# Two tiles of a scaled matrix product leave in four transfers of 6, 5, 12 and 105 rows

## The chip, the cores and the metric

The kernel runs on one core of a Trainium2 chip. A core has a matrix engine (PE), three engines for elementwise work (DVE, ACT, POOL, the last also called GpSimd), and a sequencer (SP, SyncE) that does no arithmetic and here issues transfers. Transfers between the chip's main memory (HBM) and the core's on-chip memory (SBUF, 128 partitions) are carried out by 16 DMA engines that the core's issuing engines share. The metric is the device time of one execution in microseconds; the profile's span runs from the first to the last recorded instruction and is a little shorter.

## The reference

```python
batch, m, k, n = 16, 512, 1024, 768        # all float32, scale = 0.1
def reference(x, weight, scale, add_value):
    return (scale * np.matmul(x, weight) + add_value).astype(np.float32)
```

The batch is flattened: 8192 rows of x times a 1024 by 768 weight, times 0.1, plus an array of the shape of the result.

## The kernel before

The 8192 rows are 64 tiles of 128 rows. Tiles are grouped in blocks of 24, 24 and 16, and inside a block a partition holds neighbouring rows of memory, so that a transfer of n tiles is, on each of 128 partitions, one contiguous run of n times 3 KB (of the result or the added array) or n times 4 KB (of x). A "row" of a transfer below is such a run on one partition: a transfer of two tiles of the result has 128 rows of 6 KB.

SP issues all transfers, in the order written out in STREAM. A word such as `a56+8` names the operand (x, w for weight, a for the added array, o for the result), the first tile and the number of tiles. In front of each transfer SP waits for what it needs (the helper `need`): a load for its buffer to be free, a store for the semaphore `made` to say that the tiles have been finished. Each transfer counts one semaphore up by 16 when its data have landed. The last word, `o62+2`, is left out of this loop and is issued after the block in which all engines run their programs, when all of them have reached its end.

The loaded tiles of x lie in 16 slots (`xs`). ACT and POOL each run `mover`: moves of four tiles, in which they cast x from float32 to bfloat16 into one of two buffers (`va`), each engine half of the casts, eight of them to a move and engine (sixteen half-sized ones in the first two moves). DVE transposes the result of a move, two tiles at a time, into `xt` (L190). PE multiplies: eight chunks of the contraction for each tile, a 512-wide and a 256-wide matmul for each chunk (L248, L222). DVE then scales the product, adds the loaded array and writes the sum over it in `ao` (L199), two tiles at a time, and counts `made` up. `ao` has 32 tile slots; it holds the added array first, then the result, and the stores read it.

The mover's first four moves are written out; the remaining twelve are a loop of three iterations with four moves each, in which the wait for the loaded tiles and the wait for a free `va` buffer take their values from the loop's register. POOL's last move, tiles 60 to 63, is the last move of the last iteration.

Tiles 46 and 47 are stored as part of `o32+16`, the transfer of 16 tiles late in STREAM:

```python
... x60+4 a52+4 a56+8 o32+16 o48+8 o56+6 o62+2
```

## Time and profile before

| | |
|---|---|
| time, median of 3 runs | 209.41 us (209.21 to 209.54) |
| the profiled execution's own time | 209.42 us |
| its span | 207.6 us |
| what lies around the span | 1.8 us |
| PE busy | 170.7 us (82%) |
| DVE busy | 123.0 us (59%) |
| ACT busy | 137.8 us (66%) |
| POOL busy | 138.3 us (67%) |
| packets of the hardware queue, as a share of 16 engines' span | 98.0% |

How to read it: the DMA share is a mean over the 16 DMA engines, so that one engine alone at work shows as about 0.06. A packet is one row of a transfer, or the small write by which a DMA engine reports its part of the transfer. For a stretch of time the share counts the packets that start in it. A DMA line of the profile's part on issues gives the median time from the issue to the landing of the whole transfer. Issuing a transfer is not counted as busy time of the issuing engine.

### The profile page before, as it was taken

How to read it: one execution, taken by the hardware profiler on the slowest of the kernel's cores; microseconds unless marked ns; L12 is line 12 of the kernel's file. 1: busy time of each engine (PE TensorE's matmuls, PEld its weight loads, DVE VectorE, ACT ScalarE, POOL GpSimd, SP SyncE). 2: the span in 40 equal slices, each digit the busy share in tenths (PEclk: the TensorE clock that was granted, in tenths of full speed). 3: DMA queues.
4: the chain of work that ended last, by engine and by line, in shares of the span. 5: the costliest groups of instructions: out<-in, count | busy, mean ns of one | idle time of the engine just before them, and what ended most of it. 6: DMA issues, size and time to landing. Idle time of an engine off the chain costs nothing.

```text
span 207.6 us, 2250 instructions
## 1 busy us (share of the span) xinstructions
PE 170.7 (82%) x1024; PEld 50.8 (24%) x512; DVE 123.0 (59%) x66; ACT 137.8 (66%) x145; POOL 138.3 (67%) x148
## 2 busy tenths in 40 slices
PE   0001993699999999999999999999999899999800
PEld 0000230123223333333333333333333233333200
DVE  0038304937677767776777677767774867777320
ACT  2494199999596969696969079999696959100000
POOL 0399299999797969696969179999796959200000
PEclk9999999699999999999999999999999999999995
DMA  6999999999999999899999999999999999998994
GB/s 224 458 432 410 448 455 404 455 455 404 404 473 436 420 388 505 350 421 440 436 431 447 404 450 459 404 420 436 436 421 428 412 455 469 455 445 355 434 420 173
DMA packets 4034, 87.05 MB, mean 419 GB/s; under 512 B 448, under 2 KB 448, under 8 KB 576
## 3 DMA queue, kind: packets, MB, share of 16 engines
q1 hardware_dynamic: 4032, 87.03, 98.0%
q14 instruction: 2, 0.02, 0.0%
HBM read 61.87 MB, written 25.17 MB: 419 GB/s over the span
## 4 chain that ended last, share of the span: by engine, by line
PE 59%; DMA 26%; POOL 5%; DVE 4%; issue 2%; SPq 0%; DVEq 0%; POOLq 0%
PE mm L248 39%; PE mm L222 20%; DMA xs<-in_x_dram 11%; DMA out_dram<-ao 10%; DMA ao<-in_add_value_dram 5%; POOL va L166 5%; DVE xt L190 2%; DVE ao L199 2%; SPq L99 0%; SPq L102 0%; DVEq L199 0%; DVEq L196 0%; POOLq L160 0%; DVEq L188 0%; SPq L292 0%
## 5 line engine op out<-in xcount | busy, mean ns | idle before, releaser
L248 PE MATMUL mm<-w_bf,xt 128*128 128x512 bf16 x512 | 170.3, 385 | 26.0 <-DVE w_bf L183 20.2
L166 POOL CAST va<-xs 32x1024 bf16<-32x1024 f32 (+1 forms) x144 | 138.1, 959 | 39.1 <-DMA xs<-in_x_dram 18.6
L166 ACT CAST va<-xs 32x1024 bf16<-32x1024 f32 (+1 forms) x144 | 136.5, 948 | 38.4 <-DMA xs<-in_x_dram 20.5
L222 PE MATMUL mm<-w_bf,xt 128*128 128x256 bf16 x512 | 141.4, 276 | 0.0
L199 DVE SCALAR_TENSOR_TENSOR ao<-mm,ao 128x1536 f32 (+1 forms) x32 | 56.2, 1755 | 58.7 <-PE mm L222 46.2
L248 PEld LDWEIGHTS mm<-w_bf,xt 128*128 128x128 bf16 x512 | 50.8, 99 | 145.4 <-issue 138.4
L190 DVE STREAM_TRANSPOSE xt<-va 128x1024 f32<-128x1024 f32 x32 | 65.2, 2037 | 16.9 <-POOL va L166 16.9
L183 DVE CAST w_bf<-ao 128x3072 bf16<-128x3072 f32 x2 | 4.3, 2170 | 0.0
L153 ACT ACT_TABLE_LOAD x1 | 1.3, 1283 | 1.3 <-SPq L255 1.3
L278 POOL MEMSET const-float32-0.0<- 128x1 f32 x1 | 0.1, 98 | 0.2 <-issue 0.2
L278 POOL MEMSET const-bfloat16-1.0<- 128x1 bf16 x1 | 0.1, 100 | 0.0
L278 POOL MEMSET const-uint8-127<- 128x1 uint8 x1 | 0.1, 98 | 0.0
L278 POOL MEMSET const-float32-1.0<- 128x1 f32 x1 | 0.1, 97 | 0.0
## 6 DMA issues: line engine op xcount, KB each, us to landing
xs<-in_x_dram SPq DMA_DIRECT2D x6, 4096.0 KB, 20.5
ao<-in_add_value_dram SPq DMA_DIRECT2D x7, 3072.0 KB, 17.0
out_dram<-ao SPq DMA_DIRECT2D x5, 3072.0 KB, 22.4
xs<-in_x_dram SPq DMA_DIRECT2D x4, 2048.0 KB, 14.3
out_dram<-ao SPq DMA_DIRECT2D x1, 6144.0 KB, 29.9
ao<-in_weight_dram SPq DMA_DIRECT2D x1, 3072.0 KB, 14.0
ao<-in_add_value_dram SPq DMA_DIRECT2D x2, 1536.0 KB, 9.9
out_dram<-ao SPq DMA_DIRECT2D x1, 2304.0 KB, 11.5
```

The source lines that it names most:

```text
L153: eng.preload_act_table(mybir.ActivationFunctionType.Copy)
L166: copied = copy(va[q % VA_BUFS][32 * b:32 * b + 32, t:t + step, a, :], src[32 * a:32 * a + 32, t:t + step, b, :])
L183: eng.tensor_copy(w_bf[:, s:s + n, :], ao[:, s:s + n, :]).then_inc(casts, n)
L190: eng.transpose(xt[:, 2 * half:2 * half + 2, :, :].rearrange("p i c (a m) -> p i c a m", a=4), pairs.rearrange("p i a (k c) -> p i c a k", ...
L199: eng.scalar_tensor_tensor(a, mm[:, q:q + 2, 0:N], float(scale), a, op0=mybir.AluOpType.mult, op1=mybir.AluOpType.add).then_inc(made, 2)
L222: return eng.add_instruction(mybir.InstMatmult(name=nc.get_next_instruction_name(), engine=eng.engine, ins=[eng.lower_ap(weights), eng.low ...
L248: eng.matmul(mm[:, q, 0:CUT], piece, w_bf[:, j, 0:CUT], **flags)
L278: nc = _bacc.Bacc("TRN2", target_bir_lowering=False, num_devices=1)
```

## The change

`o32+16` becomes `o32+14`. The result of tiles 46 and 47, 128 rows of 6 KB, leaves in four transfers instead, cut by partitions: the first 6 rows from SP, right behind `o32+14`; then 5, 12 and 105 rows from POOL, one after the other, between its last two moves, once `made` says that tile 47 is finished. Each of the four has a semaphore of its own, and ACT waits for all four at the end of its program. So that POOL's transfers can stand ahead of its last move, the mover's loop is turned by one move: three moves are written out ahead of it, its iterations hold the moves of slots 3, 0, 1, 2, and the last move stands behind it. The number of moves and of casts stays the same, for ACT too. SP, which issued every transfer before, shares that with POOL.

```diff
+SPREAD = 46
+SPREAD_ROWS = (("SP", 6), ("Pool", 5), ("Pool", 12), ("Pool", 105))
-    ... a52+4 a56+8 o32+16 o48+8 o56+6 o62+2
+    ... a52+4 a56+8 o32+14 o48+8 o56+6 o62+2
+    spread_sem = [tc.alloc_semaphore(f"spread{i}") for i in range(len(SPREAD_ROWS))]
+
+    def spread(eng, name):
+        first = 0
+        for (by, n), sem in zip(SPREAD_ROWS, spread_sem):
+            if by == name:
+                eng.dma_start(rows(out_v, SPREAD, 2)[first:first + n],
+                              ao[first:first + n, slots(SPREAD, 2), :]).then_inc(sem, 16)
+            first += n
+        assert first == P
...
             transfer(eng, op, s, n).then_inc(sem, 16)
+            if op == "o" and last == SPREAD:
+                need(made, MADE + SPREAD + 2)
+                spread(eng, "SP")
...
-        for q in range(X_SLOTS // MOVE):
+        for q in range(3):
             move(q, MOVE // 2 if q in HALVED else MOVE, 16,
                  MOVE * (q + 1) if q >= VA_BUFS else None)
-        with eng.Fori(32, T + 1, X_SLOTS) as i:
-            for q in range(X_SLOTS // MOVE):
-                move(q, MOVE, i, i + (4 * q - 12) if q < 3 else i)
+        with eng.Fori(16, T, X_SLOTS) as i:
+            move(3, MOVE, i, i)
+            for q in range(3):
+                move(q, MOVE, i + 16, i + 4 * (q + 1))
+        if go is not None:
+            eng.wait_ge(made, MADE + SPREAD + 2)
+            spread(eng, "Pool")
+        move(3, MOVE, T, T)
+        if go is None:
+            for sem in spread_sem:
+                eng.wait_ge(sem, 16)
```

More of the change, by code (lines that the diff above doesn't have):

```diff
@@ L20 @@
 FETCH = 128
+SPREAD = 46
+SPREAD_ROWS = (("SP", 6), ("Pool", 5), ("Pool", 12), ("Pool", 105))
 STREAM = """
     x0+4 w0+8 x4+8 a0+8 x12+4 a8+8 x16+8 a16+8 x24+8 a24+8 x32+8 o0+8 o8+8 a32+8 x40+8
-    a40+8 x48+8 x56+4 o16+8 o24+8 a48+4 x60+4 a52+4 a56+8 o32+16 o48+8 o56+6 o62+2
+    a40+8 x48+8 x56+4 o16+8 o24+8 a48+4 x60+4 a52+4 a56+8 o32+14 o48+8 o56+6 o62+2
 """
```

## The prediction

> **What bounds the kernel now.** I read the page first, then a table of stretches with the DMA share, then the packets of the last microseconds one by one. From the page:

> ```profile
> span 207.6 us, 2250 instructions
> DMA  6999999999999999899999999999999999998994
> DMA packets 4034, 87.05 MB, mean 419 GB/s; under 512 B 448, under 2 KB 448, under 8 KB 576
> q1 hardware_dynamic: 4032, 87.03, 98.0%
> ```

> The transfers fill the span: 16 DMA engines are busy 98.0% of it, and only the first and the last of the 40 slices are visibly short. The packets also tell how a transfer is shared out. 28 transfers of 128 rows would give 3584 packets; the page has 4032, and the 448 small ones are 28 x 16. So each DMA engine takes 128/16 = 8 rows of a transfer and adds one small packet.

> Stretch by stretch (start:end, length, busy times, granted clock, DMA share, GB/s):

> ```profile
> 2.00:26.00 24.00, 5.83 (x23) 1.56 (x12) 8.20 (x4) 11.30 (x19) 13.26 (x18) 1.00 1.00 424
> 100.00:140.00 40.00, 40.00 (x248) 12.06 (x124) 28.21 (x16) 31.46 (x31) 30.83 (x31) 1.00 1.00 431
> 177.00:190.00 13.00, 13.00 (x82) 3.91 (x41) 10.02 (x6) 0.45 (x1) 0.70 (x1) 1.00 1.00 433
> 190.00:198.00 8.00, 6.70 (x42) 1.88 (x20) 3.05 (x3) 0.00 (x0) 0.00 (x0) 1.00 0.99 426
> 203.40:203.80 0.40, 0.00 (x0) 0.00 (x0) 0.00 (x0) 0.00 (x0) 0.00 (x0) 0.50 1.06 445
> 203.80:204.20 0.40, 0.00 (x0) 0.00 (x0) 0.00 (x0) 0.00 (x0) 0.00 (x0) 0.50 0.95 399
> 204.20:204.60 0.40, 0.00 (x0) 0.00 (x0) 0.00 (x0) 0.00 (x0) 0.00 (x0) 0.50 0.81 338
> 204.60:205.00 0.40, 0.00 (x0) 0.00 (x0) 0.00 (x0) 0.00 (x0) 0.00 (x0) 0.50 0.38 154
> 205.00:205.20 0.20, 0.00 (x0) 0.00 (x0) 0.00 (x0) 0.00 (x0) 0.00 (x0) 0.50 0.08 31
> 205.20:205.40 0.20, 0.00 (x0) 0.00 (x0) 0.00 (x0) 0.00 (x0) 0.00 (x0) 0.50 0.07 31
> 205.40:206.20 0.80, 0.00 (x0) 0.00 (x0) 0.00 (x0) 0.00 (x0) 0.00 (x0) 0.50 0.05 23
> ```

> All engines of the DMA work without a break from 2 us to 203.8 us; then they fall out one after the other, and from 205.0 us on the share is that of one engine in 16. That one engine sets the end. Its packets, first from 205.0 us and then from 205.2 us (bins of 0.075 and 0.07 us):

> ```profile
> DMA  0100100100100100000000000000000000000000
> DMA packets 9, 0.03 MB, mean 10 GB/s; under 512 B 4, under 2 KB 4, under 8 KB 9
> DMA  0200020020020000000000000000000000000000
> DMA packets 5, 0.02 MB, mean 9 GB/s; under 512 B 1, under 2 KB 1, under 8 KB 5
> SPq L292 <- DMA out_dram<-ao: 7.5, 1, 7.5
> out_dram<-ao SPq DMA_DIRECT2D x1, 768.0 KB, 7.9
> ```

> Five rows start after 205.0 us, one behind the other; from the first to the fourth start after 205.2 us it is 10 bins for three rows, 0.23 us a row. The fifth starts at about 205.97 us and ends at about 206.20 us. The other three small packets lie between 205.0 and 205.2 us: three more engines are done only there, the other 12 earlier. The last DMA wait of SP (7.5 us, L292) is for exactly this store, `o62+2`, 7.9 us from issue to landing. So the last engine is about 206.20 - 205.15 = 1.05 us behind the next. PE, DVE, ACT and POOL do nothing in that time.

> **The change part by part.** The sum is made against the profiled execution, 209.42 us (span 207.6 and 1.8 around it), which is 0.01 from the median of 209.41.

> *What the last engine loses.* The 128 rows of tiles 46 and 47 came as 8 to each engine. The change is said to leave engine 4 three. Nothing in the profile numbers the engines, so whether the last one is engine 4 is an assumption, and so is the sharing out of the pieces; 5 rows fewer is 5 x 0.23 = 1.15 us, and the profile has just five rows alone at the end. The bounds: at most all 8 rows go (-1.84); with four pieces it may also get more (below).

> *What the others gain.* Five rows must go elsewhere. If they go singly, five engines have 9 rows, 0.23 us later. If one of the three that end by 205.2 us is among them (chance 1 - (10 x 9 x 8)/(15 x 14 x 13) = 0.74, were the five drawn from 15), the new end of the rows is about 205.15 + 0.23 = 205.38 instead of 206.20: a gain of 0.82. If none is, the last engine's own 206.20 - 1.15 = 205.05 and the others' 205.15 leave 1.05. I take 0.82, the likelier.

> [...] No run here shows a transfer of other than 128 rows.

> *Smaller rows and more packets.* Rows of 48 KB (177 to 190 us) move at 433 GB/s, the 6 KB and 18 KB ones (203.4 to 203.8 us) at 445 with whole packets counted at their start, and 24 KB ones at 426 to 433: no loss that these rows resolve. Three or four small packets more per engine, and a second queue on each engine, are not in this trace. Lower bound 0; upper bound one row per engine, 0.23 (a bubble at a change of queue can hardly be longer than a row without showing as idle, and no such idle exists in the stretches above). Nearest are the small packets, which leave the share at 1.00; I take 0.05, and the range holds 0.23.

> *POOL's three issues.* The rows that decide when they come and who waits:

> ```profile
> 158.21 8.70 POOL L166 CAST va<-xs 32x1024 bf16<-32x1024 f32 x8 [1.68 <-DVE xt L190]
> 169.00 8.70 POOL L166 CAST va<-xs 32x1024 bf16<-32x1024 f32 x8 [2.10 <-DVE xt L190]
> 154.34 1.76 DVE L199 SCALAR_TENSOR_TENSOR ao<-mm,ao 128x1536 f32 x1 [1.48 <-PE mm L222]
> 166.79 2.06 DVE L190 STREAM_TRANSPOSE xt<-va 128x1024 f32<-128x1024 f32 x1
> 170.84 1.76 DVE L199 SCALAR_TENSOR_TENSOR ao<-mm,ao 128x1536 f32 x1 [2.00 <-PE mm L222]
> 181.23 1.76 DVE L199 SCALAR_TENSOR_TENSOR ao<-mm,ao 128x1536 f32<-128x1536 f32 x1 [1.49 <-PE mm L222]
> 182.91 2.00 DVE L190 STREAM_TRANSPOSE xt<-va 128x1024 f32<-128x1024 f32 x1
> 196.80 1.76 DVE L199 SCALAR_TENSOR_TENSOR ao<-mm,ao 128x1536 f32<-128x1536 f32 x1 [3.44 <-PE mm L222]
> 161.23 0.80 SPq L104 DMA_DIRECT2D ao<-in_add_value_dram  x2
> 193.39 0.33 SPq L105 DMA_DIRECT2D out_dram<-ao  x1
> 198.84 0.33 SPq L105 DMA_DIRECT2D out_dram<-ao  x1
> DMA to landing us min/median/max: 8.6/11.3/15.5
> ```

> Counting back from the last L199 row (196.80, tiles 62 and 63) in pairs, the one at 154.34 finishes 46 and 47, at 156.1 us; the new wait on `made` is past when POOL ends its last move but one at 166.91. The last move waits for DVE until 169.00 anyway, so 2.1 us of issuing are free. Beyond that the last move is late; its first reader is the transpose at 182.91, so POOL may start it as late as 182.91 - 8.70 = 174.2: 7.3 us for three issues. An issue on SP takes 0.33; one on POOL is in no row. Between 0.33 and the 2.1 of a whole DVE operation each, three take 1 to 6.3 us: covered, cost 0. Past that point PE and then the last stores are late. Those have a cover of their own: `o62+2` is issued at 198.84 and its rows cannot start before the engines reach them, 8 x 0.23 = 1.84 us ahead of an end of 204.2 at the earliest, at 202.4; some 2.8 us, less 0.7 from issue to start, are spare.

> *The loads that POOL's rows meet.* From 167 us on they stand beside `a52+4` and `a56+8` (issued from 161.23, landing after 8.6 and 15.5 us: 169.8 and 177.1). `a52` is read at 170.84, 1.0 us later; two or three rows ahead of its end cost up to 0.7, and a slip of the DVE operation there by some tenths is inside PE's double buffer. `a56`, late by up to 8 x 0.23 = 1.84, is read at 181.23. Cost 0; if uncovered, 0.7 at most.

> *The rest.* SP's six-row issue stands behind `o32+14` and ahead of `o48+8`, which waits for `made` until 177.8 in any case: 0.33 us hidden. The turned loop makes the same 12 moves in the same order: 0, at most one fetch of code behind the loop, inside the same 7.3 us. ACT's four waits end long before 198.6, as `o32+16` landed by 192.

> ```profile
> out_dram<-ao SPq DMA_DIRECT2D x1, 6144.0 KB, 29.9
> 162.08 0.43 SPq L105 DMA_DIRECT2D out_dram<-ao  x1
> 177.82 21.35 SPq L105 DMA_DIRECT2D out_dram<-ao  x3
> ```

> (162.08 + 29.9 = 192.0.) The sum: 209.42 - 0.82 + 0.05 = 208.65, which I round to **208.6 us**, 0.4% faster. Its own range is 208.2 (1.05 gained, and the other engines' delays shrinking with it) to 208.95 (0.23 of switching cost and a next engine that was a little later).

> **Rivals.** *The three rows go to another engine than the last* (chance 0.16). The sharing out does what it says, but the late engine has 8 or 9 rows: 209.42 + 0.05 = 209.47, or 209.70 with one row more. For it: no row names the engine. Against: the fit of five rows to five rows.

> *The last engine gets more rows, and it is slower* (0.10). If GpSimd's pieces are cut into equal shares of rows per engine that begin with the same engine each time, a low-numbered engine gets 1 + 1 + 1 + 7 = 10 of the 128 rows: 209.42 + 2 x 0.23 + 0.05 = 209.93, slower by 0.24%. It decides as soon as that engine is the last one. For it: 128 rows are shared evenly now; against: nothing. [...]

> *POOL's issues hold the last move too long* (0.06). Beyond 7.3 us for the three, and beyond some 2 us of cover at the stores, each us is a us: three of 5 us would give 209.42 + 15 - 7.3 - 2.1 = 215.0. For it: POOL issues no transfer in this trace. Against: the longest DVE operation beside it is 2.06 us. [...] No run here shows a transfer issued by GpSimd.

> **How the numbers follow.** The forecast has 0.68. A change below 0.2% (0.42 us) is about what a measurement of this kernel can't tell from none. The forecast counts as faster; so does nothing else: 0.68. The first rival is mostly the same (0.14), at worst slower (0.02); the second and third, 0.16, are slower. Range 208.2 to 209.8: below lies little, above the second and third rival and part of the first.

> **What would show it.** The tail after 205 us loses its five lone rows, and the share falls from 1 to 0 within about 1.5 us. A second queue with 122 rows appears, landing by about 177 us. The gap of POOL ahead of its last move grows from 2.1 to some 3 to 6 us, DVE's transpose near 182.9 still waits for PE alone. Five or more lone rows at the end, with one engine 0.2 us or more later than now, would mean that the rows went elsewhere; idle DMA engines between 190 and 203 us, that the stores came late.

## The result, and the profile after

The changed kernel takes 210.06 us (median of 14 runs, 209.81 to 210.39) beside 209.49 us for the kernel before (14 runs): 1.0024 of it, with an interval of 1.0016 to 1.0033. The change costs 0.57 us. The forecast was 208.6 us with a range of 208.2 to 209.8 us; the time lies above it.

Of the page of the changed kernel: the span, the packets, the two queues, and POOL's row for the new transfers.

```profile
span 208.3 us, 2247 instructions
DMA packets 4238, 87.05 MB, mean 418 GB/s; under 512 B 524, under 2 KB 524, under 8 KB 780
q1 hardware_dynamic: 4044, 86.28, 96.9%
q0 software_dynamic: 192, 0.75, 0.9%
L115 POOL DMA_DIRECT2D out_dram<-ao x3 | 1.7, 575 | 0.0
```

The new queue q0 is POOL's: 0.75 MB are its 122 rows of 6 KB. The three issues take 575 ns each in the mean. The timeline of POOL around them, and then the transpose that first needs the last move:

```profile
167.60 1.70 POOL L115 DMA_DIRECT2D out_dram<-ao  x3
169.35 8.71 POOL L182 CAST va<-xs 32x1024 bf16<-32x1024 f32 x8
183.01 2.01 DVE L214 STREAM_TRANSPOSE xt<-va 128x1024 f32<-128x1024 f32 x1
```

The issues fill the gap in which POOL waited before; its last move starts at 169.35 us (169.00 before), and the transpose at 183.01 us (182.91 before). This part costs nothing.

The end of the kernel is what became longer. First come stretches of the last microseconds of the changed kernel (the last two columns are the DMA share and GB/s). Then come the packets that start after 205.4 us in bins of 0.09 us, before the change and after it:

```profile
204.20:204.60 0.40, 0.00 (x0) 0.00 (x0) 0.00 (x0) 0.00 (x0) 0.00 (x0) 0.50 1.03 430
204.60:205.00 0.40, 0.00 (x0) 0.00 (x0) 0.00 (x0) 0.00 (x0) 0.00 (x0) 0.50 0.45 184
205.00:205.40 0.40, 0.00 (x0) 0.00 (x0) 0.00 (x0) 0.00 (x0) 0.00 (x0) 0.50 0.08 31
205.40:206.00 0.60, 0.00 (x0) 0.00 (x0) 0.00 (x0) 0.00 (x0) 0.00 (x0) 0.50 0.07 31
206.00:206.40 0.40, 0.00 (x0) 0.00 (x0) 0.00 (x0) 0.00 (x0) 0.00 (x0) 0.50 0.07 31
206.40:207.00 0.60, 0.00 (x0) 0.00 (x0) 0.00 (x0) 0.00 (x0) 0.00 (x0) 0.50 0.03 10
```

```profile
DMA  0100101000000000000000000000000000000000
DMA packets 4, 0.02 MB, mean 5 GB/s; under 512 B 1, under 2 KB 1, under 8 KB 4
```

```profile
DMA  1001010010100100000000000000000000000000
DMA packets 7, 0.04 MB, mean 10 GB/s; under 512 B 1, under 2 KB 1, under 8 KB 7
```

All engines but one are done at about the same time as before, soon after 205 us. One is again last by itself, and has six lone rows after 205.4 us instead of three. Its last row starts seven bins later: 7 x 0.09 = 0.63 us, which is the loss, within a bin. The five lone rows of the forecast did not go away; some were added.

How many the last engine got can be counted. The trace records the start, length and size of each packet, but not its engine. On a busy engine each packet as a rule begins 3 or 4 ns before the recorded end of the one ahead of it, so the packets of one engine can be followed back from the last one. Two packets sometimes fit at one point; the best fit is taken here, under the condition that SP's transfers come in their order with eight rows each where they have 128. Before the change this chain has eight rows of `o32+16`. In the changed kernel it has eight of `o32+14`, one of SP's six, and one, one and seven of POOL's pieces: ten rows of tiles 46 and 47. (A chain with one more of POOL's rows fits nearly as well, but lacks the small packet that ends the last piece.)

### The profile page after: what moved, and what is told of

The parts are those of the page before. It is cut to its first block, busy times and chain, and to the rows that moved or that the text cites. A ratio compares the mean times of both kernels' runs of the same rounds, so it can differ in the third digit from the quotient of the medians.

```text
span 208.3 us, 2247 instructions
## 1 busy us (share of the span) xinstructions
PE 171.2 (82%) x1008; PEld 50.9 (24%) x512; DVE 122.6 (59%) x66; ACT 137.8 (66%) x145; POOL 140.5 (67%) x151
## 2 busy tenths in 40 slices
DMA packets 4238, 87.05 MB, mean 418 GB/s; under 512 B 524, under 2 KB 524, under 8 KB 780
## 4 chain that ended last, share of the span: by engine, by line
PE 71%; DMA 11%; POOL 7%; DVE 4%; issue 2%; SPq 0%; DVEq 0%; POOLq 0%
PE mm L272 46%; PE mm L246 25%; DMA xs<-in_x_dram 11%; POOL va L182 7%; DVE xt L214 3%; DVE ao L223 1%; SPq L101 0%; SPq L104 0%; DVEq L240 0%; POOLq L176 0%; DVEq L223 0%; DVEq L212 0%; SPq L316 0%; POOLq L190 0%; DVEq L220 0%
## 5 line engine op out<-in xcount | busy, mean ns | idle before, releaser
L272 PE MATMUL mm<-w_bf,xt 128*128 128x512 bf16 x496 | 167.3, 387 | 24.7 <-DVE w_bf L207 19.8
L207 DVE CAST w_bf<-ao 128x3072 bf16<-128x3072 f32 x2 | 3.8, 1941 | 0.0
L115 POOL DMA_DIRECT2D out_dram<-ao x3 | 1.7, 575 | 0.0
```

The costliest lines, as they stand in the source:

```text
L115: eng.dma_start(rows(out_v, SPREAD, 2)[first:first + n], ao[first:first + n, slots(SPREAD, 2), :]).then_inc(sem, 16)
L207: eng.tensor_copy(w_bf[:, s:s + n, :], ao[:, s:s + n, :]).then_inc(casts, n)
L272: eng.matmul(mm[:, q, 0:CUT], piece, w_bf[:, j, 0:CUT], **flags)
```

## Experiments

All kernels below are the changed kernel with another list of pieces for tiles 46 and 47 (one with another number of tiles); each computes the whole result. The intervals are of the ratio to the kernel before, timed beside it on the same chip. "Engine 4" is the fifth engine, counted from 0, in the order in which a piece is dealt out; no trace gives an engine's number.

**Everything but the unevenness.** First the two tiles in one transfer from POOL, then in one transfer from SP, then in four equal pieces from POOL.

```diff
-SPREAD_ROWS = (("SP", 6), ("Pool", 5), ("Pool", 12), ("Pool", 105))
+SPREAD_ROWS = (("Pool", 128),)                    # e2
+SPREAD_ROWS = (("SP", 128),)                      # e1
+SPREAD_ROWS = (("Pool", 32),) * 4                 # e12
```

> All 128 rows of tiles 46 and 47 leave in one transfer from POOL, eight to each DMA engine, none from SP. Theory 1 (every piece is dealt out from the first engine on, and the engine that ends last is among the first five, so that it got 1+1+1+7 = 10 rows): the cost is the two extra rows, so this kernel has no cost to speak of, 209.5 us (+0.0 to +0.1). Theory 2 (GpSimd's pieces go on from where the last one stopped; another engine was spared, and the last one got 9 rows, 0.23 us; the other 0.3 us is the price of the second queue): 209.8 us. Theory 3 (the whole excess is the price of POOL's queue and issues, however the rows are dealt out): 210.0 us.

> All 128 rows of the two tiles in one transfer from SP, with the store of 14 tiles ahead of it and the turned loop; nothing from POOL, nothing uneven. All theories: the cutting of the store and the turned loop cost nothing, 209.4 to 209.5 us.

> Four pieces as in the changed kernel, but of 32 rows each and all from POOL: two rows of each piece to every engine, eight in all, nothing uneven. Theory 1 (the uneven sharing out is the cost; a piece more costs 0.03 to 0.05 us): 209.4 + 0.1 = 209.5 us, at most 209.6. If four pieces and a second queue are themselves the cost: 210.0 us.

Measured: 209.37 us (ratio 0.9990 to 1.0008), 209.46 us (0.9992 to 1.0011) and 209.46 us (0.9994 to 1.0012). Every interval holds 1, and none reaches beyond 0.25 us. So the turned loop, the cut store, POOL's issues and a second queue cost nothing that can be measured, and neither do four pieces from POOL of which every engine gets eight rows. Theory 3, a price of the queue, falls. The last kernel's packets after 205.4 us are those of the kernel before, each row one bin (0.09 us) earlier:

```profile
DMA  1001010000000000000000000000000000000000
DMA packets 4, 0.02 MB, mean 5 GB/s; under 512 B 1, under 2 KB 1, under 8 KB 4
```

**Which engine, and from where a piece is dealt out.** Two kernels with the same number of pieces from POOL, 112 rows and four small ones. If each piece starts at the first engine, pieces of 4 leave engine 4 with 7 rows and pieces of 5, 5, 5 and 1 give it 10. If pieces go on where the last one stopped, every engine has 8 in both.

```diff
+SPREAD_ROWS = (("Pool", 112), ("Pool", 4), ("Pool", 4), ("Pool", 4), ("Pool", 4))   # e6
+SPREAD_ROWS = (("Pool", 112), ("Pool", 5), ("Pool", 5), ("Pool", 5), ("Pool", 1))   # e7
```

> All 128 rows from POOL, as 112 (seven to each engine) and four pieces of 4 rows. Theory 1 (each piece is dealt out from the first engine on; the engine that ends last is the fifth, engine 4): engines 0 to 3 get 11 rows, all others 7, the last one loses one row: 209.42 - 0.23 = 209.2 us. Theory 2 (each piece goes on where the last one stopped): all engines get 8, 209.4 us. If the last engine is one of the first four: 210.1 us.

> The same number of pieces from POOL, 112, 5, 5, 5 and 1 rows. Theory 1: engine 0 gets 11, engines 1 to 4 get 10, all others 7; engine 4, the last, has two rows more, as in the changed kernel: 209.42 + 0.46 = 209.9 us, 0.7 us above the kernel with pieces of 4 rows. Theory 2: pieces of 5, 5, 5 and 1 rows go once around all 16 engines, eight rows each: 209.4 us, no difference to the pieces of 4. If the last engine is the sixth or a later one: 209.2 us.

Measured: 209.33 us (0.9987 to 1.0005) and 210.09 us (1.0023 to 1.0052), 0.76 us apart; theory 1 had 0.69, theory 2 nothing. Their packets after 205.4 us, pieces of 4 and then pieces of 5:

```profile
DMA  0101000000000000000000000000000000000000
DMA packets 4, 0.01 MB, mean 3 GB/s; under 512 B 2, under 2 KB 2, under 8 KB 4
```

```profile
DMA  1001001010010100000000000000000000000000
DMA packets 8, 0.04 MB, mean 10 GB/s; under 512 B 2, under 2 KB 2, under 8 KB 8
```

With pieces of 4 the last row starts three bins (0.27 us) earlier than before, about one row's worth; that execution was one of the two fastest of eleven, and the medians differ by 0.11 us. With pieces of 5 it starts seven bins later, as in the changed kernel. The chain that ends last has seven of POOL's rows with pieces of 4, and ten with pieces of 5. The piece of 1 row did not go to one engine: the trace has it as 16 packets of 384 bytes, of which this chain has one. So each of POOL's pieces of several rows is dealt out from the first engine on, and the engine that ends last is the only one that a piece of 5 reaches and a piece of 4 does not: engine 4. The change had the right engine. Counted by this rule, its four pieces give that engine 1 + 1 + 1 + 7 = 10 rows, the ten of its chain: one, one and one of the pieces of 6, 5 and 12, and seven of the 105.

**Twice the dose.**

```diff
+SPREAD_ROWS = (("Pool", 96), ("Pool", 5), ("Pool", 5), ("Pool", 5), ("Pool", 5), ("Pool", 5), ("Pool", 5), ("Pool", 2))
```

> Pieces of 96, six times 5, and 2 rows from POOL: engine 4 gets 6 + 6 = 12 rows, four more than before, engines 5 to 15 six. Theory 1, with a row at 0.23 us: 209.44 + 0.92 + 0.1 to 0.2 for the pieces = 210.5 us, twice the step of the kernel with 5, 5, 5 and 1. If the step there was a fixed price of such pieces and not one by rows: 210.1 us.

Measured: 210.67 us (1.0051 to 1.0078) beside 209.38, 1.29 us more; theory 1 had 1.0 to 1.1, a fixed price 0.7. The chain that ends last has 12 of POOL's rows. It goes by rows, and a little more than by rows: above 0.23 a row the excess is 0.37 us here (eight pieces), 0.19 with 5, 5, 5 and 1 (five pieces), 0.12 with the pieces of 4 (-0.11 measured, -0.23 by rows) and 0.11 in the change (four pieces). That is some 0.02 to 0.05 us a piece, but four equal pieces cost less than can be measured, so what the remainder is stays open.

**The same pieces from SP, and why they are dearer.** The change's four pieces all from SP; 112 rows and four pieces of 4 with the large or all pieces from SP; and eight pieces of 16 rows from SP, in which nothing is uneven.

```diff
+SPREAD_ROWS = (("SP", 6), ("SP", 5), ("SP", 12), ("SP", 105))                           # e3
+SPREAD_ROWS = (("SP", 112), ("SP", 4), ("SP", 4), ("SP", 4), ("SP", 4))                 # e4
+SPREAD_ROWS = (("SP", 112), ("Pool", 4), ("Pool", 4), ("Pool", 4), ("Pool", 4))         # e5
+SPREAD_ROWS = (("SP", 16),) * 8                                                         # e8
```

> The same four pieces of 6, 5, 12 and 105 rows, all issued by SP, none by POOL. Theory 1: the same sharing out as in the changed kernel, two extra rows for the last engine, 0.46 us and a little for more packets: 209.95 to 210.05 us. Theory 3: no queue of POOL, no cost: 209.5 us. Theory 2 says nothing certain of SP's pieces; with nine rows 209.75 us.

> SP issues 112 rows (seven to each engine) and four pieces of 4 rows. If pieces are dealt out from the first engine on, engines 0 to 3 get 11 rows and all others 7. If the engine that ends last is one of 0 to 3, it has three rows more: 209.5 + 0.69 = 210.2 us. If it is engine 4 or a later one, it has one row less: 209.5 - 0.23 + 0.05 = 209.3 us, as long as the first four, 0.69 us later, still end ahead of it.

> As the kernel with SP's four pieces of 4 rows, but the four pieces come from POOL. Theory 1 (each piece starts at the first engine): engines 0 to 3 get 11 rows, the others 7, and the time moves the same way as with SP's pieces, 209.3 or 210.2 us. Theory 2 (each piece goes on where the last one stopped): every engine gets 7 + 1 = 8 rows, no change beyond the queue's price: 209.5 to 209.8 us. Theory 3: 210.0 us.

> SP issues eight pieces of 16 rows: every engine gets eight rows, but in each piece the 16 engines read 16 neighbouring partitions at the same time. If the 1.03 us of SP's four uneven pieces are more than two rows (0.46) because rows that are read close together hold each other up, this kernel is slower although nothing is uneven: 209.7 to 210.4 us, and rows longer than 0.23 us. If the excess there was in the sharing out alone: 209.4 to 209.5 us.

Measured: 210.45 us (1.0034 to 1.0060), 209.92 us (1.0017 to 1.0041), 210.41 us (1.0032 to 1.0070) and 211.24 us (1.0082 to 1.0114). The first speaks against theory 3, but is 1.03 us above the kernel before where the rows account for 0.46. The second and third hit none of the expected values, and their times by themselves decide nothing. The fourth shows that the share of rows is not all: with eight rows for every engine, by the count, it is the slowest of all, 1.80 us above the kernel before. Here is the stretch in which its pieces run, first before the change, then with all 128 rows in one transfer from SP, then with the pieces of 16:

```profile
188.00:193.00 5.00, 5.00 (x33) 1.54 (x16) 3.49 (x3) 0.00 (x0) 0.00 (x0) 1.00 1.00 433
```

```profile
188.00:193.00 5.00, 5.00 (x33) 1.47 (x15) 3.49 (x3) 0.00 (x0) 0.00 (x0) 1.00 1.02 433
188.00:193.00 5.00, 5.00 (x33) 1.47 (x15) 3.48 (x3) 0.00 (x0) 0.00 (x0) 1.00 1.02 320
```

The engines are as busy, but move 320 instead of 433 GB/s: (433 - 320) x 5 us is 0.57 MB, or 1.3 us at the old rate. The rows themselves became longer: 41 of the 128 took more than 249 ns, up to 1907, and together 19.9 us over the usual 234 ns, which is 1.24 us an engine. In one transfer from SP none took more than 248 ns. What holds them up was not shown: the 16 rows of such a piece lie in neighbouring partitions, they go to places 72 KB apart in memory, and there are eight transfers instead of one. In the kernel with the change's pieces from SP, two or three engines are late (0.15 x 16 = 2.4) instead of one:

```profile
205.40:206.00 0.60, 0.00 (x0) 0.00 (x0) 0.00 (x0) 0.00 (x0) 0.00 (x0) 0.50 0.15 61
206.00:206.40 0.40, 0.00 (x0) 0.00 (x0) 0.00 (x0) 0.00 (x0) 0.00 (x0) 0.50 0.15 61
```

Longer rows are behind those 0.57 us too. The chain that ends last there has ten rows, by the same sharing out, and they took 0.57 us more than 234 ns each; two of them alone took 359 and 618 ns. With SP's 112 rows and POOL's pieces of 4, the chain that ends last has seven of SP's rows, of 234 to 784 ns, and none of POOL's. With all five pieces from SP, 16 of the 128 rows were longer than 249 ns, up to 871. In the changed kernel no row of POOL's took more than 252 ns: the same four pieces cost 1.03 us from SP and 0.57 with three of them from POOL. POOL's pieces are not always spared: one of the 128 rows took 521 ns with four pieces of 32, and more did in the next two kernels.

**Trying for a gain.** More taken from engine 4: 96 rows and eight pieces of 4; then longer rows, of three tiles (`SPREAD_TILES` also stands in place of 2 where the pieces are issued and waited for).

```diff
+SPREAD_ROWS = (("Pool", 96),) + (("Pool", 4),) * 8                                     # e9
-SPREAD = 46
+SPREAD = 45                                                                            # e10
+SPREAD_TILES = 3
+SPREAD_ROWS = (("Pool", 112), ("Pool", 4), ("Pool", 4), ("Pool", 4), ("Pool", 4))
-... o32+14 ...
+... o32+13 ...
```

> All rows from POOL, 96 (six to each engine) and eight pieces of 4 rows. Theory 1: engines 0 to 3 get 14 rows, 1.38 us more than before, all others 6; the last engine ends 0.46 us earlier, at about 205.75 us of the span, and the first four at 203.8 to 205.15 before, now 205.2 to 206.5: 209.0 us if they were early ones, 209.7 us if one of them was the last but one. Theory 2: 209.4 us.

> As the kernel with POOL's pieces of 112, 4, 4, 4 and 4 rows, but of tiles 45, 46 and 47: rows of 9 KB, 0.345 us each. Theory 1 (dealt out from the first engine on, engine 4 ends last): engine 4 loses one longer row, 0.345 us, the first four gain three; with the 0.13 us that the five pieces cost above the count of rows there, 209.44 - 0.345 + 0.13 = 209.2 us. If the first four have become the end: 209.4 us or more.

Measured: 209.48 us (0.9992 to 1.0010) and 209.97 us (1.0013 to 1.0031). Neither gains. The DMA share near the end is the same in both (the first kernel's profile is of its slowest execution, 209.81 us):

```profile
205.00:205.40 0.40, 0.00 (x0) 0.00 (x0) 0.00 (x0) 0.00 (x0) 0.00 (x0) 0.50 0.33 138
205.40:206.00 0.60, 0.00 (x0) 0.00 (x0) 0.00 (x0) 0.00 (x0) 0.00 (x0) 0.50 0.27 113
```

A share of 0.27 to 0.33 is four or five engines (4.3 to 5.3 of 16), where the kernel before has one. By the count, the four engines that take the rows have joined the end, or become it: the chain that ends last has 14 of POOL's rows in the first and 11 in the second. The first lies between its two expected values. The second missed its expected 209.2 us and met its other case. Three rows of 9 KB are 1.04 us, less than the 1.39 us of six rows of 6 KB, but in its last chain three rows together took 1.27 us more than the usual 347 ns each; the longest in that trace took 1124 ns. In the first kernel ten of POOL's rows were longer than 249 ns, up to 499. No kernel here beats the kernel before by what can be measured; the pieces of 4 rows come nearest, at 0.9996.

## Why the prediction was wrong

- *What bounds the kernel* held. The transfers do, at 98.0% of the span, and at the end one DMA engine alone, 1.05 us behind the next by the prediction's bins and 1.09 by the last packets (206.25 and 205.16 us). Every kernel that gave this engine more rows became slower, and three of the four that left it its eight did not; the fourth, with pieces of 16 rows, lost its time in longer rows.
- *What the last engine loses* is the step that failed: "the change is said to leave engine 4 three" was taken as a term, -1.15 us, of which 0.82 went into the sum. No run shows that term. The runs showed +2 rows in its place, 0.46 us by the row and 0.57 measured. That the last engine is engine 4, the assumption beside it, was right. The sharing out was not: the chain that ends last has 1 + 1 + 1 + 7 rows where three were forecast, as it must if a piece starts at the first engine each time.
- The second rival was the outcome: ten rows, 209.93 us forecast and 210.06 measured, with the mechanism and the point as it stood there. It was given 0.10, though the prediction names nothing against it. What it held against the first rival was that five lone rows and five rows taken away looked like a fit. That fit said which number the change aimed at, not that its pieces would be dealt out so. The trace had no transfer of other than 128 rows, so nothing in it spoke for the one rule or the other. The kernels with pieces of 4 and of 5 rows did: 0.76 us apart, they agree with pieces that each start at the first engine (0.69 expected), and not with pieces that go on where the last one stopped (no difference expected).
- *What the others gain* had its arithmetic on the wrong engines; by the same rule the first four were given two extra rows each as well, but end early enough not to show: the share after 205.4 us is 0.07, one engine of 16. With the pieces of 4 even three extra rows each did not show (209.33 us); six brought them to the end, and so did three of 9 KB, which took longer than usual.
- *Smaller rows and more packets*, 0.05 us with 0.23 as the bound: POOL's four equal pieces cost less than can be measured (0.9994 to 1.0012), and its uneven ones 0.11 to 0.37 us beyond their rows. That rows of SP's pieces took up to 1907 ns instead of 234 was in no term; in the changed kernel no row of POOL's took more than 252 ns.
- *POOL's three issues* held: 1.70 us in all, inside the forecast 1 to 6.3, at no cost. The 2.1 us for one issue, a whole DVE operation, was an estimate; the three took 521 to 643 ns. One working there does not come out: from the issue at 198.84 us to 202.4 us are 3.6 us, which less 0.7 leaves 2.9, where the rival on POOL's issues used 2.1. The 0.7 us from issue to start has no row there; in the trace before, the first load's issue ends at 1.32 us and its first row starts at 1.95, 0.63 us later. Nothing hung on it. The second queue's rows landed later than the 177 us that were expected, by their rows in the list of issues (size, us to landing):

```profile
out_dram<-ao POOLq DMA_DIRECT2D x1, 630.0 KB, 19.1
out_dram<-ao POOLq DMA_DIRECT2D x1, 72.0 KB, 7.6
out_dram<-ao POOLq DMA_DIRECT2D x1, 30.0 KB, 6.2
```

Issued from 167.6 to 168.7 us, the largest is done at 187.8 us. Seven rows of 0.23 us are 1.6 us of work for an engine, but they stood among those of the other queue. In the chain that ends last, POOL's rows start 1.85 to 1.86 us apart between 177.6 and 185.1 us: one row of 6 KB, then one of `o32+14`, 42 KB in about 1.6 us. The loads beside them came in time: DVE's operation on `a52` started at 170.94 us, 170.84 before:

```profile
170.94 1.76 DVE L223 SCALAR_TENSOR_TENSOR ao<-mm,ao 128x1536 f32 x1 [1.77 <-PE mm L246]
```

## What to carry to other kernels

Here the DMA engines were busy for 98.0% of the span, and the time was that of the engine that ended last: with two rows of 6 KB more it ended 0.6 us later, and the kernel took 0.57 us more. So how a transfer is dealt out over the engines was part of its price. Pieces with a count of rows that 16 divides cost nothing measurable from POOL (128 rows, or four times 32), but such a count was not safe by itself: SP's eight pieces of 16 rows made the slowest kernel (211.24 us). Before a change is built on which engine gets which row, run a pair of kernels that differ in that alone: pieces of 4 and of 5 rows told both the rule and the engine. A number in the profile that fits an intention is no evidence that the mechanism exists.
